# Sample state update in other PSUM banks, a third state buffer, a first chunk without its zero state, and later loads in the last group

## The chip, the cores and the metric

The kernel runs on one core of a Trainium2 chip. The metric is the device time of one execution in microseconds; lower is better. Engines are named as in the profile: PE (matmul) with PEld (its weight loads), DVE (vector), ACT (scalar), POOL (GpSimd) and SP, which only issues DMAs here. ACT issues some DMAs too.

## What is computed

One layer of a hybrid encoder, for a prompt of 2048 frames and for 8 running streams of 16 frames each (the sample). Cut to what matters:

```python
h = rmsnorm(x);  P = h @ w_in                    # q|k|v, z, b, a, B, C, H
# group A, gated delta rule, 4 heads of 128, in chunks; S is the state, zero at the prompt's start
v_new = u - w @ S
o     = (q*exp(g)) @ S + qk @ v_new
S     = S * a_last + k_tail.T @ v_new
o     = rmsnorm(o) * silu(z)
# group B, short convolution
y     = B * causal_dwconv3(C * H)
x     = x + rmsnorm(concat(o, y) @ w_o)
x     = x + rmsnorm((silu(h2 @ w_gate) * (h2 @ w_up)) @ w_down)
```

The sample starts from given states (`state`, 8 streams x 4 heads x 128 x 128) and returns the new ones; the prompt starts from zero.

## The kernel before

The rows are cut into 17 tiles of 128: 0 to 15 are the prompt, 16 is the sample. `GROUPS` puts them into five groups, `[0..3]`, `[4..7]`, `[8..10]`, `[11, 12, 16]`, `[13..15]`. For each group a loop over 28 weight blocks (slots) multiplies the group's rows by one 128-column block of `w_in`, 24 matmul rows per slot (L317: each product is made of three, from a high and a low part), into one of three `dbank`s. A slot has three thirds, and between thirds the loop runs *events*: short pieces of the delta rule, whose times are written in the table `PLAN` (event number = 3 x slot + third). Events past 84 run in the next group. PE's order is what the code says (`manual_schedule`); the other engines, and SP's DMAs, are ordered by a scheduler that simulates the kernel, unless `issue_after` ties an instruction behind another.

The eight PSUM banks of this phase are three `dbank` (blocks), two `tbank` (transposes), two `gbank` and one `obank` (delta rule). Each name is a ring: the next user waits until the last reader of that bank has finished.

- `fetch` / `weights`: SP loads weight block j (1024 KB, from `wsplit`, L287) into a ring of three; a load waits until PE is through with the block three slots back.
- `gate_decay`, `decay_mask`, `decay_scale`: the cumulated decays of a group are turned (L557), written to DRAM by ACT (`grow`, L561), and read back by SP, broadcast over the partitions, into `dt` (L563); DVE adds masks (L569), ACT takes the exponential (L572), DVE scales (L576). `pair_keys` (L592 on PE, L593 on DVE) uses `dt`.
- `chunk`: one prompt tile of the delta rule: products with S (L739, L747), with the solved U (L755), the new S (L761, L764) and the output (L769, L770); `out_norm`, `out_turn` (L720, L722) finish it. The first chunk of the prompt runs the same code on `S_init`, which DVE zeroes at the start.
- `sample_head`: one head of the sample. Its state `st` (512 KB) is loaded by SP (L793), multiplied (L806), solved (L812), used (L816), and updated: four matmuls (L824) into four banks, `pss = [bank(), bank(), obank(), tbank()]`, then eight DVE operations (L826) that read two halves of each bank; ACT stores it (L828).
- `ahead`: in the last group, loads the first quarter of `w_o` and the first output tile's inputs into parts of `U`, `AU`, `dt`, `kt`, `vt`, `sz` that are free (256 KB each, L905 to L909). The event is at 64, but the scheduler may place the issues earlier.

After the five groups come the output projection (L1116), the gated up-projection (L1351) and the down-projection (L1528).

Of the kernel before, what the change touches and what calls it, by code (L numbers as in the profile page):

```python
# [9 lines left out]
F32 = mybir.dt.float32  # L10
# [7 lines left out]
P = 128  # L18
D = 1024
KD = D // P  # L20
H = 4
# [4 lines left out]
NS = 8  # L26
# [6 lines left out]
MAXT = max(len(g) for g in GROUPS)  # L33
# [19 lines left out]
NR, NKV, NACC = 3, 2, 3  # L53
XKB = 6
NHX = 1
NWB = 12
NDA = 6
NDR = 4
# [32 lines left out]
def kernel(  # L91
# [66 lines left out]
    with ExitStack() as ph:  # L158
# [6 lines left out]
        def obank():  # L165
            return pso.tile([P, 512], F32, tag="o", name="obank")

        def tbank():
            return pst.tile([P, 512], F32, tag="t", name="tbank")

        def bank():
            return psg.tile([P, 512], F32, tag="g", name="gbank")

        S_init = gp.tile([P, H, P], F32, tag="S", name="S_init", bufs=2)
        V.memset(S_init, 0.0)
        now = {"S": S_init}
        junko = gp.tile([P, P], BF16, name="junko")
        masks = gp.tile([P, 648], F32, name="masks")
        tri_p, tri_s, blk_s, smask, neg_p, neg_s = (masks[:, a - 256:b - 256] for a, b in list(CONSTS.values())[2:])
# [207 lines left out]
        def finish_block(j, ps, g):  # L387
            tiles, n, rb = g["tiles"], g["n"], g["rb"]
            c = n * P
            pc = g["npr"] * P  # L390
            kind, h = BLOCKS[j]
            if kind == "k":
                o = gp.tile([P, W1], F32, tag="kT", name="kT", bufs=H)
                conv_qkv(tiles, 4 + h, ps, o, rb)
                g["kT"].append(o)

                def later():
                    tb, t3 = turned(o, n)
                    sumsq(tb, n, g["ssk"], h)
                    A.copy(g["kt"][:, h, :n], t3)  # L400
                return later
            if kind == "q":
                o = gp.tile([P, W1], F32, tag="qT", name="qT", bufs=H)
                conv_qkv(tiles, h, ps, o, rb)
                g["qT"].append(o)

                def later():
                    tb, _ = turned(o, n)
                    sumsq(tb, n, g["ssq"], h)
                return later  # L410
            if kind == "v":
                raw = cp.tile([P, W1], F32, tag="vraw", name="vraw", bufs=NKV)
                conv_qkv(tiles, 8 + h, ps, raw, rb)

                def later():
                    _, t3 = turned(raw, n)
                    for i in range(n):
                        A.activation(g["vt"][:, h, i], t3[:, i], AF.Copy, scale=g["rt"][:, 4 * i + h:4 * i + h + 1])
                return later
            if kind == "z":  # L420
                src = ps[:, :c]
                if rb is not None:
                    src = g["sz"][:, h, :c]
                    V.tensor_mul(src, ps[:, :c], rb[:, :c])
                mark["A"] = A.activation(g["sz"][:, h, :c], src, AF.Silu)
                flush(mark["A"])
            w = scw[:, h, :]
            v = lambda a: sl(a[:, pc:c])
            if kind == "C":
                g["cs"] = cs = cp.tile([P, W1], F32, tag="cs", name="cs")  # L430
                if rb is None:
                    flush(A.copy(cs[:, :c], ps[:, :c]))
                else:
                    V.tensor_mul(cs[:, :c], ps[:, :c], g["rb2"][:, :c])
            if kind == "H":
                cs = g["cs"]
                g["acc"] = acc = cp.tile([P, WF], F32, tag="acc", name="acc", bufs=NACC)
                u = cp.tile([P, 3 + WF], F32, tag="R", name="u", bufs=NR)
                f = pc
                G.tensor_copy(u[:, 0:2], shist[:, h, :])  # L440
                V.tensor_mul(u[:, 2:2 + pc], cs[:, :pc], ps[:, :pc])
                G.tensor_copy(shist[:, h, :], u[:, pc:pc + 2])
                if pc < c:
                    f = pc + NS * (2 + LS)
                    us = segments(u, pc, 2, 2 + LS)
                    V.tensor_copy(us[:, :, 0:2], sch[:, h])
                    V.tensor_mul(us[:, :, 2:], v(cs), v(ps))
                    V.tensor_copy(sch[:, h], us[:, :, LS:LS + 2])
                mark["A"] = A.activation(acc[:, :f], u[:, 2:2 + f], AF.Copy, scale=w[:, 2:3])
                mark["V"] = taps(acc[:, :f], lambda d: u[:, d:d + f], w, 3)  # L450
            if kind == "B":
                acc = g["acc"]
                last = h == 3 and g["gi"] + 1 == len(GROUPS)
                yo = wk.tile([P, W1], F32, tag="ye", name="yo") if last else cp.tile([P, W1], F32, tag="cs", name="yo")
                V.tensor_mul(yo[:, :pc], acc[:, :pc], ps[:, :pc])
                if pc < c:
                    V.tensor_mul(v(yo), segments(acc, pc, 0, 2 + LS)[:, :, 2:], v(ps))
                if rb is not None:
                    V.tensor_mul(yo[:, :c], yo[:, :c], rb[:, :c])
                if last:  # L460
                    last_stores.append((mixs[g["gi"]][:, h, :], yo[:, :c]))
                else:
                    nc.scalar.dma_start(out=mixs[g["gi"]][:, h, :], in_=yo[:, :c])
# [89 lines left out]
        def gate_decay(g):  # L553
            n, nG = g["n"], g["nG"]
            m = 4 * n
            ps = bank()
            T.transpose(ps[:m, :P], nG[:, :m], ident)  # L557
            rw = small.tile([4 * MAXT, P], F32, tag="rw", name="rw", bufs=1)
            V.tensor_scalar_mul(rw[:m], ps[:m, :P], -1.0)
            grow = dram.tile([4 * MAXT, P], F32, name=f"grow{g['gi']}")  # L560
            nc.scalar.dma_start(out=grow[:m], in_=rw[:m])  # L561
            g["dt"] = dt = gp.tile([P, MAXT, H, P], F32, tag="dt", name="dt")
            nc.sync.dma_start(out=dt[:, :n].rearrange("p t h c -> p (t h) c"), in_=grow[:m].partition_broadcast(P))  # L563

        def decay_mask(g, i):
            dt, nG, t = g["dt"], g["nG"], g["tiles"][i]
# [161 lines left out]
        def tail_keys(g, i):  # L728
# [2 lines left out]
                A.activation(kl[:, h], g["kt"][:, h, i], AF.Copy, scale=g["tl"][:, 4 * i + h:4 * i + h + 1])  # L731
            return kl

        def chunk(g, i):
            c = slice(i * P, (i + 1) * P)
            S = now["S"]
# [52 lines left out]

        def sample_head(g, i, h):  # L790
            c = slice(i * P, (i + 1) * P)
            st = wk.tile([P, NS, P], F32, tag="st", name="st", bufs=2)
            tc.keep_in_program_order(nc.sync.dma_start(out=st, in_=state[:, h].rearrange("s k v -> k s v")))  # L793
            yield
            kz, qz, kl, r, yt, o = (smp[nm] for nm in ("kz", "qz", "kl", "r", "yt", "o"))
# [22 lines left out]
            ye = smp["ye"]  # L818
            V.tensor_mul(ye, yt[h].unsqueeze(1).broadcast_to([P, 2, P]), smp["pair"].unsqueeze(2).broadcast_to([P, 2, P]))
            yield  # L820
            pss = [bank(), bank(), obank(), tbank()]
            for j, ps in enumerate(pss):
                r_ = slice(32 * j, 32 * j + 32)
                T.matmul(ps[:, :2 * P], kl[r_, h, :], ye[r_].rearrange("p s v -> p (s v)"), start=True, stop=True)  # L824
# [15 lines left out]
        def plan(g, nx, events):  # L840
# [33 lines left out]
                at(u + 10, lambda: out_norm(g, npr, smp["o"]))  # L874
                at(u + 17, lambda: out_turn(g, npr, smp["o"]))
            for i in range(npr):
                thread((t, t + 2, t + 4, t + 10), chunk(g, i))
                t += 6
            if nx is not None:
                tiles = GROUPS[gi + 1]  # L880
                m = len(tiles)
                for i in range(m):
                    at(43 + 4 * i, x_rows_load, tiles, i, nx)
                    at(46 + 4 * i, x_rows, i, nx)
                b = 47 + 4 * m + (0 if gi else 3)
                at(b - 3, x_factors, tiles, nx)
                at(b, x_spread, tiles, nx)
                ts = [62, 65, 68, 69, 70, 71, 72, 73]
                for k in range(KD):
                    at(ts[k], x_load, tiles, k, nx)  # L890
                    if k < NHX:
                        at(max(ts[k], b) + 5, x_norm, tiles, k, nx)
                        at(max(ts[k], b) + 6, x_split, tiles, k, nx)
                    else:
                        at(max(ts[k], b) + 6, x_norm, tiles, k, nx)

            else:
                at(64, ahead, g)

        def ahead(g):  # L900
            kt, vt, sz = (g[nm][:, :, MAXT - 1] if nm != "sz" else g[nm][:, :, W1 - P:] for nm in ("kt", "vt", "sz"))
            early_w[:] = [(U[:, MAXT - 1], AU[:, MAXT - 1]), (g["dt"][:, MAXT - 1], kt)]
            for k, halves in enumerate(early_w):
                for q, v in enumerate(halves):
                    nc.sync.dma_start(out=v, in_=w_o[k, :, 512 * q:512 * q + 512].rearrange("p (h c) -> p h c", h=H))  # L905
            early_m[:] = [vt, sz]
            nc.sync.dma_start(out=vt, in_=mixo[0])
            gi, i = PLACE[0]
            nc.sync.dma_start(out=sz, in_=mixs[gi][:, :, i * P:(i + 1) * P])  # L909

        def next_rows(gi, nx):
            tiles = GROUPS[gi]
# [77 lines left out]
        matmuls(firsts[2], pending[2][1:], hi, lo, c, range(6))  # L990
        rb = spread(rg, n)
        matmuls(firsts[2], pending[2][1:], hi, lo, c, range(6, KD))
        rb2 = wk.tile([P, NS, P], F32, tag="st", name="rb2", bufs=2).rearrange("p s v -> p (s v)")[:, :W1]
        G.memset(U, 0.0)

        def constants():
# [727 lines left out]
```

## Time and profile before

| | us |
|---|---|
| median of 3 runs | 2456.97 (2456.92 to 2458.26) |
| span of the profiled execution, first to last instruction | 2457.2 |
| PE busy | 2428.1 |
| DVE busy | 1619.9 |
| ACT busy | 1045.7 |
| POOL busy | 578.6 |

No time of the profiled execution other than its span is listed; the span lies 0.2 us above the median. PE is the engine that sets the time: what it does not do is 29 us. Groups 0 to 4 run to about 860 us (chunk 0 at 173 us, the sample from about 650 to 742 us), the output projection and gated up-projection to about 1980 us, the down-projection to the end. The mean granted clock of PE is 0.998.

### The profile page before, as it was taken

Reading aid. Unit: us, or ns where it says so; the run is one execution under the profiler, and the core shown is the slowest. Engines: PE = TensorE matmul, PEld = TensorE weight load, DVE = VectorE, ACT = ScalarE, POOL = GpSimd, SP = SyncE. Lnnn points to the kernel's source line nnn. Section 1 sums busy time; section 2 is a strip of 40 time slices with the busy share of each in tenths; the row PEclk is TensorE's granted clock in tenths of the full one; section 3 lists DMA queues with packets and bytes.
Section 4 is the critical chain, followed back from the end, with each engine's and each line's share of the span. In section 5 each row is a group of like instructions: output and inputs, shape, how many; then the busy total and the mean of one; then the engine's idle time right before and its main releaser. Section 6 shows DMA issues by size and latency. Waiting matters only on the chain.

```text
span 2457.2 us, 39354 instructions
## 1 busy us (share of the span) xinstructions
PE 2428.1 (99%) x14376; PEld 2222.2 (90%) x14376; DVE 1619.9 (66%) x3079; ACT 1045.7 (43%) x2338; POOL 578.6 (24%) x664
## 2 busy tenths in 40 slices
PE   9999999999999999999999999999999999999997
PEld 7888889999989978899999999999999988887886
DVE  7875755746667366788888644556555565677698
ACT  6545546546444343444444422324333345333343
POOL 1101001001110000156655200000000046455563
PEclk9999999999999999999999999999999999999999
DMA  7774655666776466598877788778898743333465
GB/s 272 262 246 163 220 194 203 244 222 232 273 261 234 162 222 225 195 336 301 289 268 259 266 261 266 252 246 273 307 298 283 249 144 118 116 111 122 132 224 191
DMA packets 263465, 561.38 MB, mean 228 GB/s; under 512 B 25188, under 2 KB 144680, under 8 KB 245992
## 3 DMA queue, kind: packets, MB, share of 16 engines
q1 hardware_dynamic: 146864, 486.98, 57.3%
q10 hardware_dynamic: 116184, 70.85, 9.5%
q8 instruction: 113, 1.85, 0.3%
q0 software_dynamic: 224, 1.05, 0.1%
q14 instruction: 80, 0.66, 0.1%
HBM read 400.09 MB, written 158.70 MB: 227 GB/s over the span
## 4 chain that ended last, share of the span: by engine, by line
PE 87%; DVE 6%; DMA 2%; issue 2%; POOL 2%; ACT 1%; SPq 0%; DVEq 0%; ACTq 0%; POOLq 0%
PE fbank L1351 36%; PE dbank L317 26%; PE fbank L1528 11%; PE dbank L1116 4%; PE tbank L1116 4%; POOL dw L1201 1%; DVE xr L1551 1%; PE tbank L375 1%; DVE acc L1488 1%; PE gbank L592 1%; PE gbank L599 1%; PE obank L769 1%; POOL as L1511 1%; PE obank L747 1%; PE gbank L739 1%
## 5 line engine op out<-in xcount | busy, mean ns | idle before, releaser
L1351 PE MATMUL fbank<-xh,fw 128*128 128x384 f32 (+1 forms) x3696 | 898.1, 326 | 2.7 <-ACT m L1385 2.5
L317 PE MATMUL dbank<-hi,w 128*128 128x384 f32 (+1 forms) x2240 | 655.6, 363 | 2.2 <-DMA w<-wsplit 1.4
L1351 PEld LDWEIGHTS fbank<-xh,fw 128*128 128x128 f32 x3696 | 651.6, 188 | 3.4 <-ACT m L1385 2.8
L1351 PE MATMUL fbank<-xl,fw 128*128 128x384 f32 (+1 forms) x1848 | 602.4, 326 | 0.0
L317 PEld LDWEIGHTS dbank<-hi,w 128*128 128x128 f32 x2240 | 412.6, 188 | 43.9 <-issue 4.0
L1528 PE MATMUL fbank<-dw,as 128*128 128x512 f32 x1782 | 420.2, 392 | 3.4 <-DVE as L1511 1.2
L1528 PEld LDWEIGHTS fbank<-dw,as 128*128 128x128 f32 x1782 | 332.9, 188 | 82.1 <-POOL as L1511 3.5
L317 PE MATMUL dbank<-lo,w 128*128 128x384 f32 (+1 forms) x1120 | 399.6, 357 | 0.3 <-DVE lo L232 0.3
L1351 PEld LDWEIGHTS fbank<-xl,fw 128*128 128x128 f32 x1848 | 347.3, 188 | 0.0
L317 PEld LDWEIGHTS dbank<-lo,w 128*128 128x128 f32 x1120 | 210.7, 188 | 16.6 <-DVE lo L232 0.6
L1511 POOL TENSOR_TENSOR as<-ar,as 128x256 fp32r<-128x256 f32 (+1 forms) x202 | 184.2, 924 | 171.1 <-ACT as L1508 168.7
L1488 DVE TENSOR_TENSOR acc<-acc,fbank 128x512 f32<-128x512 f32 x248 | 164.9, 681 | 90.2 <-PE fbank L1528 77.1
L1201 POOL TENSOR_TENSOR dw<-dr,dw 128x512 fp32r<-128x512 f32 x48 | 70.3, 1477 | 497.5 <-ACT dw L1199 497.3
L1508 ACT CAST as<-ar 128x256 fp32r<-128x256 f32 (+1 forms) x287 | 116.4, 427 | 166.8 <-PE fbank L1528 124.3
L1326 ACT CAST fw<-rg 128x512 fp32r<-128x512 f32 x124 | 77.2, 622 | 228.6 <-PE fbank L1351 138.3
L321 DVE SCALAR_TENSOR_TENSOR acc<-R,vec,acc 128x512 f32<-128x512 f32 (+2 forms) x180 | 120.9, 672 | 27.0 <-ACT acc L358 20.8
L1399 DVE TENSOR_TENSOR c<-u,fbank 128x384 f32<-128x384 f32 (+1 forms) x66 | 34.8, 528 | 95.5 <-PE fbank L1351 95.5
L1395 DVE TENSOR_TENSOR m<-m,m 128x384 f32<-128x384 f32 (+1 forms) x44 | 23.1, 525 | 82.8 <-ACT m L1385 82.8
L1327 POOL TENSOR_TENSOR fw<-rg,fw 128x512 fp32r<-128x512 f32 x44 | 65.3, 1485 | 45.9 <-ACT fw L1326 41.9
L1397 ACT ACTIVATE m<-fbank 128x384 f32<-128x384 f32 (+1 forms) x66 | 31.2, 473 | 96.4 <-PE fbank L1351 79.0
L350 POOL COPY hist<-R 128x3 f32<-128x3 f32 x60 | 20.1, 335 | 220.6 <-ACT R L326 171.5
L1402 ACT ACTIVATE c<-c 128x384 f32<-128x384 f32 (+1 forms) x66 | 33.4, 507 | 83.4 <-DVE c L1401 83.4
(395 smaller groups left out, 3575.6 us busy)
## 6 DMA issues: line engine op xcount, KB each, us to landing
w<-wsplit SPq DMA_DIRECT2D x105, 1024.0 KB, 4.9
fw<-fsplit SPq DMA_DIRECT2D x188, 512.0 KB, 4.8
fsplit<-fw SPq DMA_DIRECT2D x94, 512.0 KB, 3.6
partd<-pt ACTq DMA_DIRECT2D x86, 384.0 KB, 6.1
rg<-in_w_gu SPq DMA_DIRECT2D x62, 512.0 KB, 4.0
wsplit<-w SPq DMA_DIRECT2D x28, 1024.0 KB, 4.9
wr<-in_w_in SPq DMA_DIRECT2D x34, 512.0 KB, 5.8
ar<-partd SPq DMA_DIRECT2D x43, 384.0 KB, 3.1
```

The costliest lines, as they stand in the source:

```text
L317: T.matmul(ps[:, :c], l[:, k, :], r[k][:, :c], start=(k == 0 and r is hi and l is wh), stop=(k == KD - 1 and l is wl))
L321: r = V.scalar_tensor_tensor(acc, raw(d), w[:, d:d + 1], acc, op0=ALU.mult, op1=ALU.add)
L1116: T.matmul(pss[n], m_[:, j, :], w_[k][:, n * 512:(n + 1) * 512], start=(k == 0 and ci == 0), stop=(k == KD - 1 and ci == 2))
L1201: e.tensor_tensor(out=w[1], in0=v, in1=w[0].bitcast(F32), op=ALU.subtract)
L1326: A.copy(w[:, 0], v)
L1327: e.tensor_tensor(out=w[:, 1], in0=v, in1=w[:, 0].bitcast(F32), op=ALU.subtract)
L1351: T.matmul(ps, w_[:, c], b_[k][:, :hw], start=(first and k == 0 and ci == 0), stop=(k == KH - 1 and ci == 2), skip_group_check=not first)
L1399: V.tensor_add(c21, u2, b3)
L1488: return eng.tensor_tensor(out=dst, in0=dst, in1=ps, op=ALU.add)
L1508: ins = A.copy(a[:, 0, :n], v)
L1511: e.tensor_tensor(out=a[:, 1, :n], in0=v, in1=a[:, 0, :n].bitcast(F32), op=ALU.subtract)
L1528: T.matmul(ps, a[:, x_, q * P:(q + 1) * P], w[y_], start=(start and q == 0 and ci == 0), stop=(q == c - 1 and ci == 2), skip_group_check=True)
```

## The change

Five edits:

1. The sample's update uses one `gbank`, both `tbank`s and one `dbank` instead of two `gbank`s, the `obank` and one `tbank`. The first chunk of the sample's group turns its output two events later.
2. The state ring `st` has three buffers instead of two; the last output block `yo` uses that ring too.
3. The first chunk has a function of its own, `first_chunk`, without the two products with S and with copies where the zero state was scaled and added. `S_init` goes.
4. In the last group the decay broadcast is issued by an event of its own, `decay_load`, three events after `gate_decay` and tied behind the newest weight load.
5. `ahead` runs as six events (40, 44, ... 60), one load each, tied behind the newest weight load.

```diff
+NST = 3
...
-        S_init = gp.tile([P, H, P], F32, tag="S", name="S_init", bufs=2)
-        V.memset(S_init, 0.0)
-        now = {"S": S_init}
+        now = {"S": None}
...
-                yo = wk.tile([P, W1], F32, tag="ye", name="yo") if last else cp.tile([P, W1], F32, tag="cs", name="yo")
+                yo = wk.tile([P, NS * P], F32, tag="st", name="yo", bufs=NST)[:, :W1] if last else cp.tile([P, W1], F32, tag="cs", name="yo")
...
-            nc.sync.dma_start(out=dt[:, :n].rearrange("p t h c -> p (t h) c"), in_=grow[:m].partition_broadcast(P))
+            if g["gi"] + 1 < len(GROUPS):
+                decay_load(g)
+
+        def decay_load(g):
+            n = g["n"]
+            with tc.issue_after(wloads[-1].ins) if g["gi"] + 1 == len(GROUPS) else ExitStack():
+                nc.sync.dma_start(out=g["dt"][:, :n].rearrange("p t h c -> p (t h) c"), in_=g["grow"][:4 * n].partition_broadcast(P))
...
+        def first_chunk(g):
+            o = wk.tile([P, H, P], F32, tag="o", name="o", bufs=2)
+            kl = tail_keys(g, 0)
+            yield
+            ps = bank()
+            for h in range(H):
+                T.matmul(ps[:, h * P:(h + 1) * P], U[:, 0, h, :], g["vt"][:, h, 0], start=True, stop=True)
+            yt = wk.tile([P, H, P], F32, tag="yt", name="yt")
+            A.copy(yt, h4(ps))
+            yield
+            ps = bank()
+            for h in range(H):
+                T.matmul(ps[:, h * P:(h + 1) * P], kl[:, h, :], yt[:, h, :], start=True, stop=True)
+            now["S"] = gp.tile([P, H, P], F32, tag="S", name="S", bufs=2)
+            V.tensor_copy(now["S"], h4(ps))
+            ps = obank()
+            for h in range(H):
+                T.matmul(ps[:, h * P:(h + 1) * P], g["dt"][:, 0, h, :], yt[:, h, :], start=True, stop=True)
+            A.copy(o, h4(ps))
+            out_norm(g, 0, o)
+            yield
+            out_turn(g, 0, o)
+            yield
...
-            st = wk.tile([P, NS, P], F32, tag="st", name="st", bufs=2)
+            st = wk.tile([P, NS, P], F32, tag="st", name="st", bufs=NST)
...
-            pss = [bank(), bank(), obank(), tbank()]
+            pss = [bank(), tbank(), tbank(), psd.tile([P, 512], F32, tag="d", name="dbank")]
...
-                thread((t, t + 2, t + 4, t + 10), chunk(g, i))
+                thread((t, t + 2, t + 4, t + (12 if npr < n and not i else 10)), chunk(g, i) if gi or i else first_chunk(g))
...
-                at(64, ahead, g)
+                at(decay + 3, decay_load, g)
+                for q in range(6):
+                    at(40 + 4 * q, ahead, g, q)
```

How this stands in the queues. First PE, where the first head of the sample is updated while the chunk before it is still running (about 682 us), before:

```order
L317 MATMUL dbank<-hi,w_7152 128x384
L824 MATMUL gbank<-dt,AU 128x256 x2
L824 MATMUL obank<-dt,AU 128x256
L824 MATMUL tbank<-dt,AU 128x256
L720 MATMUL tbank<-cst,o 128x128 x4
L761 MATMUL gbank<-yt,kl 128x128 x4
L769 MATMUL obank<-yt,dt 128x128 x4
L317 MATMUL dbank<-hi,w_7195 128x384
```

The same place now (L853 is the update, L790 and L798 are the chunk's last two products, L316 the blocks; the chunk's turn, L720 above, comes after the next head's first products):

```order
L316 MATMUL dbank<-hi,w_7128 128x384
L853 MATMUL gbank<-dt,AU 128x256
L853 MATMUL tbank<-dt,AU 128x256 x2
L853 MATMUL dbank<-dt,AU 128x256
L790 MATMUL gbank<-yt,kl 128x128 x4
L798 MATMUL obank<-yt,dt 128x128 x4
L316 MATMUL dbank<-hi,w_7171 128x384
```

The turn moved back, and the update left the `obank` and one `gbank` to the chunk. Then SP in the last group, from the weight block of slot 4 on (names: `wsplit` is a weight block, `in_w_o`, `mixo` and `mixs` are the early loads, `grow` the decays), before:

```order
L287 DMA w2_7765<-wsplit8_90 128x2048
L907 DMA vt_7660<-mixo0_60 128x4x128
L287 DMA w2_7825<-wsplit9_91 128x2048
L287 DMA w2_7893<-wsplit10_92 128x2048
L905 DMA AU_200<-in_w_o 128x512
L905 DMA dt_8058<-in_w_o 128x512
L287 DMA w2_7964<-wsplit11_93 128x2048
L287 DMA w2_8034<-wsplit12_94 128x2048
L563 DMA dt_8058<-grow4_8056 128x1536
L909 DMA sz_7661<-mixs0_77 128x4x128
L287 DMA w2_8111<-wsplit13_95 128x2048
L287 DMA w2_8153<-wsplit14_96 128x2048
```

The same stretch now:

```order
L286 DMA w2_7741<-wsplit8_90 128x2048
L286 DMA w2_7801<-wsplit9_91 128x2048
L286 DMA w2_7869<-wsplit10_92 128x2048
L286 DMA w2_7940<-wsplit11_93 128x2048
L286 DMA w2_8010<-wsplit12_94 128x2048
L286 DMA w2_8086<-wsplit13_95 128x2048
L568 DMA dt_8034<-grow4_8032 128x1536
L286 DMA w2_8129<-wsplit14_96 128x2048
```

The early loads left this stretch, and the broadcast moved behind `wsplit13`. The early loads (L939, L941) now stand here, some ten slots later on SP:

```order
L286 DMA w2_8413<-wsplit7_89 128x2048
L939 DMA U_197<-in_w_o 128x512
L286 DMA w2_8476<-wsplit16_98 128x2048
L286 DMA w2_8535<-wsplit17_99 128x2048
L939 DMA AU_198<-in_w_o 128x512
L286 DMA w2_8588<-wsplit18_100 128x2048
L939 DMA dt_8034<-in_w_o 128x512
L286 DMA w2_8622<-wsplit19_101 128x2048
L939 DMA kt_7635<-in_w_o 128x4x128
```

They are six loads spread between weight blocks; the last two (vt, sz) follow in the same manner.

More of the change, by code (lines that the diff above doesn't have):

```diff
@@ L561, in gate_decay @@
             nc.scalar.dma_start(out=grow[:m], in_=rw[:m])
-            g["dt"] = dt = gp.tile([P, MAXT, H, P], F32, tag="dt", name="dt")
-            nc.sync.dma_start(out=dt[:, :n].rearrange("p t h c -> p (t h) c"), in_=grow[:m].partition_broadcast(P))
+            g["dt"], g["grow"] = gp.tile([P, MAXT, H, P], F32, tag="dt", name="dt"), grow
+            if g["gi"] + 1 < len(GROUPS):
[4 more added lines that the diff above has]
+                nc.sync.dma_start(out=g["dt"][:, :n].rearrange("p t h c -> p (t h) c"), in_=g["grow"][:4 * n].partition_broadcast(P))
         def decay_mask(g, i):
@@ L897, in plan, with ahead @@
             else:
-                at(64, ahead, g)
-        def ahead(g):
+                at(decay + 3, decay_load, g)
+                for q in range(6):
+                    at(40 + 4 * q, ahead, g, q)
+        def ahead(g, q):
             kt, vt, sz = (g[nm][:, :, MAXT - 1] if nm != "sz" else g[nm][:, :, W1 - P:] for nm in ("kt", "vt", "sz"))
             early_w[:] = [(U[:, MAXT - 1], AU[:, MAXT - 1]), (g["dt"][:, MAXT - 1], kt)]
-            for k, halves in enumerate(early_w):
-                for q, v in enumerate(halves):
-                    nc.sync.dma_start(out=v, in_=w_o[k, :, 512 * q:512 * q + 512].rearrange("p (h c) -> p h c", h=H))
             early_m[:] = [vt, sz]
-            nc.sync.dma_start(out=vt, in_=mixo[0])
             gi, i = PLACE[0]
-            nc.sync.dma_start(out=sz, in_=mixs[gi][:, :, i * P:(i + 1) * P])
+            with tc.issue_after(wloads[-1].ins):
+                if q < 4:
+                    c = slice(512 * (q % 2), 512 * (q % 2) + 512)
+                    nc.sync.dma_start(out=early_w[q // 2][q % 2], in_=w_o[q // 2, :, c].rearrange("p (h c) -> p h c", h=H))
+                else:
+                    nc.sync.dma_start(out=early_m[q - 4], in_=mixs[gi][:, :, i * P:(i + 1) * P] if q > 4 else mixo[0])
         def next_rows(gi, nx):
@@ L992 @@
         matmuls(firsts[2], pending[2][1:], hi, lo, c, range(6, KD))
-        rb2 = wk.tile([P, NS, P], F32, tag="st", name="rb2", bufs=2).rearrange("p s v -> p (s v)")[:, :W1]
+        rb2 = wk.tile([P, NS, P], F32, tag="st", name="rb2", bufs=NST).rearrange("p s v -> p (s v)")[:, :W1]
         G.memset(U, 0.0)
```

## The prediction

> **What bounds the kernel now.** I read four views in this order: the page, the waits of TensorE (PE), the stretches of 50 us, and the order of time around each wait that the change touches. The page first: the engines' busy time.
> ```profile
> PE 2428.1 (99%) x14376; PEld 2222.2 (90%) x14376; DVE 1619.9 (66%) x3079; ACT 1045.7 (43%) x2338; POOL 578.6 (24%) x664
> ```
> PE is busy for 2428.1 of 2457.2 us, so a change can only pay by issuing fewer matmuls or by closing some of the 29 us in which PE stands. The waits of PE say what it stands for; columns are total us, times, longest.
> ```profile
> PE dbank L317 <- DMA w<-wsplit: 1.4, 1, 1.4
> PE gbank L806 <- DVE st L826: 1.2, 1, 1.2
> PE gbank L761 <- DVE st L826: 1.1, 1, 1.1
> PE gbank L806 <- DMA st<-in_state: 0.6, 1, 0.6
> PE obank L769 <- DVE st L826: 0.4, 1, 0.4
> PE fbank L1528 <- DVE as L1511: 0.9, 1, 0.9
> PE fbank L1528 <- DVE acc L1488: 0.8, 1, 0.8
> ```
> The first five lie in the groups with the sample and after it, 1.4 + 1.2 + 1.1 + 0.6 + 0.4 = 4.7 us, and each names a thing that the diff edits. The last two are in the first down-projection chunk (1980 to 2060 us), which the diff does not edit. The stretches agree (first column after the comma: PE busy out of 50).
> ```profile
> 650.00:700.00 50.00, 48.52 (x384) 45.93 (x383) 24.78 (x73) 17.83 (x57) 6.49 (x19) 1.00 0.74 247
> 700.00:750.00 50.00, 48.22 (x358) 44.29 (x357) 33.42 (x94) 26.42 (x58) 7.73 (x22) 1.00 0.82 275
> 750.00:800.00 50.00, 48.53 (x347) 47.85 (x346) 36.81 (x106) 23.01 (x48) 2.09 (x10) 1.00 0.60 218
> 800.00:850.00 50.00, 50.00 (x446) 48.72 (x445) 17.67 (x45) 18.23 (x57) 2.75 (x6) 1.00 0.53 186
> ```
> Holes are 1.48, 1.78 and 1.47 us, then none. After 850 us the same PE-bound work follows, so what PE wins here should stay won.
>
> **First chunk without its zero state.** Eight of PE's calls go, recorded as 16 matmuls (each fp32 one twice).
> ```profile
> 173.31 1.06 PE L739 MATMUL gbank<-S_init,kT 128*128 128x128 f32 x8
> 174.20 1.06 PE L747 MATMUL obank<-S_init,qT 128*128 128x128 f32 x8
> 175.01 0.48 PE L317 MATMUL dbank<-hi,w 128*128 128x512 f32 x1
> 178.50 1.05 PE L755 MATMUL gbank<-r,U 128*128 128x128 f32 x8
> 173.76 0.68 DVE L704 TENSOR_SCALAR U<-gbank 64x512 f32<-64x512 f32 x1
> ```
> From start to start they hold PE from 173.31 to 175.01: 1.7 us, on the path since nothing waits there, so -1.7. What was behind them moves up: the product with U starts at 178.50 - 1.7 = 176.8, and its last input is written by DVE at 173.76 + 0.68 = 174.4, 2.4 us earlier. The DVE and ACT work that goes with the zero state (r, four scalings of o, four updates of S, for one copy each of S and o) and the memset lie beside PE: nothing. Were that cover gone, the 1.7 would shrink by what U came late.
>
> **Sample update in other banks.** Before, one head's update took both g banks, the single o bank and one t bank; now one g, both t and one d bank.
> ```profile
> 682.26 0.48 PE L824 MATMUL gbank<-dt,AU 32*128 32x256 f32 x2
> ...
> 682.91 0.66 PE L720 MATMUL tbank<-cst,o 128*128 128x128 f32 x4
> 684.68 1.13 PE L761 MATMUL gbank<-yt,kl 128*128 128x128 f32 x8 [1.11 <-DVE st L826]
> 686.18 1.13 PE L769 MATMUL obank<-yt,dt 128*128 128x128 f32 x8 [0.37 <-DVE st L826]
> ...
> 702.75 0.65 PE L806 MATMUL gbank<-st,kz 128*32 128x128 f32 x16 [1.22 <-DVE st L826]
> ```
> At these places the next products need a g or o bank that DVE has not read out, because its queue is full there. In the new order the chunk's products find the other g bank and the o bank untouched, and the next head's L806 finds a g bank last read by L817. So -1.11 - 0.37 - 1.22 = -2.7. What is late next? A t bank: the chunk's turn L720 needs one, but is moved two events behind, and DVE had the whole update done by 686.6:
> ```profile
> 685.95 0.60 DVE L826 SCALAR_TENSOR_TENSOR st<-st,eLs,tbank 128x128 f32<-128x128 f32 x2
> 682.93 0.41 DVE L455 TENSOR_TENSOR yo<-acc,dbank 128x256 f32<-128x256 f32 x1
> 758.55 4.18 PE dbank L317 x24
> ```
> And the d banks: of three, one is lent to the sample, so a block's bank must be read out within one block of 24 rows (4.18 us) instead of two. The block that ends just before 682.26 is read by DVE from 682.93, under 2 us after its end. Price: nothing up to 1.2 (the longest wait on L826 seen); I take nothing, nearest that row of 2 us against 4.18.
>
> **Third state buffer.** The load of the fourth head's state waited for a store.
> ```profile
> SPq L793 <- DMA out_state_s<-st: 7.3, 1, 7.3
> 716.93 0.64 PE L806 MATMUL gbank<-st,kz 128*32 128x128 f32 x16 [0.56 <-DMA st<-in_state]
> ```
> With three buffers it takes the first head's, stored a head earlier, so SP need not stand 7.3 us: the state can be asked for as much earlier than it was, lands before PE wants it at 716.93 - 0.56, and -0.56 follows. The weight loads behind it on SP also go out earlier. The buffer for the last output row block moves into the same ring and is free by then: nothing.
>
> **Decay broadcast and early loads.** On SP, in the last group, w13 is the weight block from wsplit13. The chain of waits reads:
> ```profile
> 742.51 0.32 SPq L563 DMA_DIRECT2D dt<-grow  x1
> 743.57 0.55 SPq L909 DMA_DIRECT2D sz<-mixs  x1
> 744.22 8.40 DMA w<-wsplit
> 752.75 0.41 PE L317 MATMUL dbank<-hi,w 128*128 128x384 f32 x1 [1.40 <-DMA w<-wsplit]
> ```
> w13 stood behind the broadcast and behind the early load of sz, and then took 8.40 us, sharing the queues with both. Now it goes ahead of the broadcast, and sz comes some twelve weight blocks later. PE wanted w13 at 752.75 - 1.40 = 751.35, and its buffer is free two blocks of 4.18 earlier, at 743.0 (an estimate); the weight loads of this stretch land after 6.4 us (next fence), so at 749.4, and even 8.40 would be in time. So -1.40. What is late next is dt, which now queues behind 1024 KB:
> ```profile
> DMA packets 8170, 18.22 MB, mean 260 GB/s; under 512 B 557, under 2 KB 5821, under 8 KB 6543
> ...
> w<-wsplit SPq DMA_DIRECT2D x12, 1024.0 KB, 6.4
> 747.38 1.14 DVE L569 SCALAR_TENSOR_TENSOR dt<-dt,nG,masks 128x128 f32<-128x128 f32 x4 [0.41 <-DMA dt<-grow]
> 750.27 2.18 DVE L569 SCALAR_TENSOR_TENSOR dt<-dt,nG,masks 128x128 f32<-128x128 f32 x8
> 757.99 1.29 DVE L593 TENSOR_TENSOR AU<-gbank,dt 128x512 f32<-128x512 f32 x2
> 763.23 1.06 PE L592 MATMUL gbank<-kT 128*128 128x128 f32 x8
> ```
> 1024 + 768 KB at the 260 GB/s of that stretch are 7.1 us: from 743.0 to 750.1 instead of 747.3. The masks (1.14 + 2.18) then end at 753.4 instead of 752.4, and L593, whose first product freed its g bank at about 758.7, does so at 759.7. PE asks for that bank at 763.23 - 1.40 = 761.8: 2.1 us to spare, so nothing. At the worst, with w13's 8.40 and then dt's own 4.9 (742.51 to 747.38) one after the other, dt lands at 756.3, the masks end 7.2 later than before, and PE waits 758.7 + 7.2 - 761.8 = 4.1 us. The six early loads (256 KB each, 1.0 us at 260 GB/s, and about 0.5 us of SP to issue, as sz's 0.55) move between the weight loads of 785 to 845 us, where DMA runs at 186 GB/s and PE has no hole: nothing, with a bound of six times 1.0.
>
> The Trainium skill (DMA: Bandwidth & Descriptors, Queues, rings and completion order) says that each DMA engine consumes descriptors in ring order; by that rule dt's bytes follow w13's, which is the 750.1 above and never w13 and dt sharing the rate from the start. The trace agrees so far as w13 behind dt took 8.40. Taken strictly it speaks against this part: what w13 wins, dt loses, which is the first rival below.
>
> **The sum**: -1.7 - 2.7 - 0.6 - 1.4 = -6.4. After a wait the first matmul also takes longer to start up (1.4 us from the last transposes' pace to L761 where 1.11 is booked), some 0.3 at one or two places, so -6.5. The order of the first down-projection chunk changes a little too (ACT and DVE casts swap; an input load passes a weight load), around the two waits of 0.9 and 0.8: between -1.7 and, if both double, +1.7; I take nothing. The profiled span 2457.2 is 0.2 above the median 2456.97, so I take the sum from 2457.0: **2450.5 us**.
>
> **Rivals.** *The late dt takes over* (rival 1): PE waits at the third pair-keys product, 0 to 4.1 us; taken at 2.5, 2453.0. For it: dt is now behind w13. Against: the 2.1 us of cover, and that the AU and dt loads of w_o no longer run just ahead. *Banks* (rival 2): the d or t bank becomes the wait, each of the four heads losing up to the 1.2 seen, so half the 2.7 or all of it comes back: 2453.2 at most 2454. Against: the 4.18 us of a block. *Early loads starve the weights* (rival 3, slower): seven weight loads stand next to an early load between 785 and 845 us; if each landed like w13 and PE waited 1.4 for each, 9.8 us are lost, 2457.0 - 6.5 + 9.8 = 2460.3. It decides when a weight lands later than two blocks after its issue, 2 x 4.18 = 8.4 us; w13 with 1024 KB ahead of it took exactly that, and these have 256 KB ahead, so I give it little. *Absorbed* (rival 4): the first down-projection chunk's new order gives back its 1.7 or more: 2452.2.
>
> **How the numbers follow.** Forecast 0.62, rival 1 0.12, rival 2 0.08, rival 4 0.14, rival 3 0.04. The forecast's own range is 2448.6 (all startup gaps and the 1.7 of the chunk won) to 2452.2; eight in ten are held by 2447.8 to 2453.6. A measurement of this kernel can tell about 0.2%, 4.9 us, from no change. Faster by more than that means below 2452.1: the forecast nearly whole, and half of rivals 1 and 4, 0.72; within it 0.25; slower 0.03.
>
> **What would show it.** Right: no L739 or L747 on a zero state near 173 us; no wait of PE on L826; none on the state's load; L317 near 750 us without a wait on wsplit; holes of 650 to 800 us below 1 us together. Wrong: a new wait of PE on a d or t bank, on DVE's AU (L593), or on wsplit between 785 and 845 us, or more than 1.7 us of PE waits between 1980 and 2060 us.

## The result and the profile after

Over 22 runs of each kernel on the same chips the median went from 2457.49 us (2454.35 to 2467.16) to 2456.51 us (2450.38 to 2460.86). The ratio is 0.9984, with a 95% interval of 0.9976 to 0.9991: 3.9 us faster, between 2.2 and 5.9. The two medians are only 1.0 us apart, the means of the same runs 3.6 (2458.6 and 2455.0), because the changed kernel's times fall into two groups and its median lies in the upper one; the ratio is near the means. It is a gain, but a smaller one than the 0.2% that the prediction drew as its line. The profiled execution took 2450.9 us (span 2449.1).

The page's line of busy times and the waits of PE in the changed kernel follow. Its line numbers differ: L855 was L826, L845 was L816, L835 was L806, L727 was L722, L477 was L478, L1560 was L1528, L1383 was L1351.

```profile
PE 2425.0 (99%) x14360; PEld 2220.6 (91%) x14360; DVE 1616.3 (66%) x3070; ACT 1047.5 (43%) x2335; POOL 579.5 (24%) x664
```
```profile
PE fbank L1560 <- DVE acc L1520: 3.5, 3, 1.7
...
PE gbank L477 <- DVE st L855: 0.8, 1, 0.8
PE gbank L845 <- ACT qT L842: 0.6, 1, 0.6
```

The 16 matmul records of the zero state are gone. None of the five waits that the change aimed at is left: no wait on `wsplit`, none on the state's load, none of the chunk's two products or of the next head's on the update. But two new ones stand among the sample's heads, 0.8 + 0.6 us: the next group's gate products (L477) wait for the update, and the sample's output product (L845) waits for `yt`, the answer that ACT copies at L842 (the profile gives that row the name of another tile, qT). In the stretches the holes fell from 1.48, 1.78 and 1.47 us to 0.62, 0.81 and 0.07:

```profile
650.00:700.00 50.00, 49.38 (x416) 46.14 (x414) 25.23 (x74) 17.22 (x56) 6.47 (x19) 1.00 0.76 257
700.00:750.00 50.00, 49.19 (x337) 45.96 (x332) 34.80 (x100) 27.82 (x60) 8.07 (x23) 1.00 0.80 263
750.00:800.00 50.00, 49.93 (x446) 49.25 (x445) 37.63 (x105) 22.44 (x48) 2.27 (x11) 1.00 0.67 235
```

To compare kernels I split each span by the starts of PE's rows. *Groups* is from the first to the last block product (L317/L316), *gate-up* from the last output-projection product to the last gate-up product, *down* from there to the last row (a row can hold several products). *Sample* is the part of the groups from the first head's products with its state to the last head's update. The time is the median of the runs, or the one run, and a ratio is to runs of the kernel before on the same chip. Every kernel of the table is described below.

| | groups | sample | gate-up | down | time | ratio, 95% interval |
|---|---|---|---|---|---|---|
| before | 853.7 | 59.5 | 918.7 | 460.0 | 2457.49 | |
| e12_before | 855.2 | 59.4 | 914.5 | 460.0 | 2455.76 | |
| after | 848.6 | 57.6 | 914.5 | 461.1 | 2456.51 | 0.9984, 0.9976 to 0.9991 |
| e11_after | 848.3 | 57.5 | 921.4 | 459.7 | 2456.29 | |
| e1_first | 852.7 | 60.6 | 921.8 | 460.1 | 2457.41 | 1.0003, 0.9994 to 1.0012 |
| e2_banks | 851.1 | 56.9 | 915.2 | 460.2 | 2455.18 | 0.9998, 0.9985 to 1.0010 |
| e3_ring | 853.2 | 58.8 | 916.2 | 459.3 | 2457.52 | 1.0002, 0.9991 to 1.0014 |
| e4_loads | 851.8 | 59.4 | 915.7 | 460.2 | 2454.70 | 0.9994, 0.9983 to 1.0004 |
| e5_two | 849.1 | 57.4 | 915.2 | 460.9 | 2451.63 | |
| e6_free | 849.0 | 58.0 | 915.2 | 460.6 | 2453.45 | 0.9984, 0.9974 to 0.9993 |
| e7_decay | 851.6 | 59.1 | 916.3 | 460.7 | 2455.22 | |
| e8_early | 853.2 | 59.5 | 915.2 | 460.7 | 2455.84 | |
| e9_turn | 848.2 | 56.5 | 915.1 | 461.3 | 2451.43 | 0.9985, 0.9976 to 0.9994 |
| e10_both | 846.6 | 55.7 | 921.4 | 459.9 | 2454.46 | 0.9985, 0.9974 to 0.9995 |

The groups, which the change edits, are 5.1 to 6.9 us shorter, depending on which of the two profiles of before is set against which of after. The gate-up stretch, which no kernel here edits, takes anything from 914.5 to 921.8 us, and hides that in the totals.

### The profile page after: what moved, and what is told of

It reads as the page before. It is cut to its first block, busy times and chain, and to the rows that moved or that the text cites. A ratio compares the mean times of both kernels' runs of the same rounds, so it can differ in the third digit from the quotient of the medians.

```text
span 2449.1 us, 39308 instructions
## 1 busy us (share of the span) xinstructions
PE 2425.0 (99%) x14360; PEld 2220.6 (91%) x14360; DVE 1616.3 (66%) x3070; ACT 1047.5 (43%) x2335; POOL 579.5 (24%) x664
## 4 chain that ended last, share of the span: by engine, by line
PE 88%; DVE 5%; DMA 2%; issue 2%; POOL 2%; ACT 1%; DVEq 0%; ACTq 0%; SPq 0%; POOLq 0%
PE fbank L1383 36%; PE dbank L316 26%; PE fbank L1560 11%; PE dbank L1148 4%; PE tbank L1148 4%; DVE xr L1583 1%; DVE acc L1520 1%; PE tbank L374 1%; POOL dw L1233 1%; PE gbank L597 1%; PE gbank L604 1%; DMA dr<-in_w_dn 1%; PE ftbank L1177 1%; PE obank L776 1%; PE gbank L768 1%
## 5 line engine op out<-in xcount | busy, mean ns | idle before, releaser
L1383 PE MATMUL fbank<-xh,fw 128*128 128x384 f32 (+1 forms) x3696 | 897.2, 326 | 0.2 <-ACT m L1416 0.2
L316 PE MATMUL dbank<-hi,w 128*128 128x384 f32 (+1 forms) x2240 | 655.3, 363 | 1.1 <-DVE w L296 0.5
L1383 PEld LDWEIGHTS fbank<-xh,fw 128*128 128x128 f32 x3696 | 651.1, 188 | 0.6 <-ACT m L1416 0.5
L1383 PE MATMUL fbank<-xl,fw 128*128 128x384 f32 (+1 forms) x1848 | 601.8, 326 | 0.0
L316 PEld LDWEIGHTS dbank<-hi,w 128*128 128x128 f32 x2240 | 412.6, 188 | 42.2 <-issue 3.6
L1560 PE MATMUL fbank<-dw,as 128*128 128x512 f32 x1782 | 419.9, 392 | 4.4 <-DVE acc L1520 2.4
L1560 PEld LDWEIGHTS fbank<-dw,as 128*128 128x128 f32 x1782 | 332.9, 188 | 83.0 <-ACT as L1540 4.7
L316 PE MATMUL dbank<-lo,w 128*128 128x384 f32 (+1 forms) x1120 | 399.6, 357 | 0.5 <-DVE lo L231 0.5
L1383 PEld LDWEIGHTS fbank<-xl,fw 128*128 128x128 f32 x1848 | 346.9, 188 | 0.0
L316 PEld LDWEIGHTS dbank<-lo,w 128*128 128x128 f32 x1120 | 210.7, 188 | 16.8 <-DVE lo L231 0.8
L1417 ACT COPY m<-fbank 128x384 f32<-128x384 f32 (+1 forms) x66 | 30.7, 464 | 75.8 <-PE fbank L1383 73.7
```

Source lines behind the costliest of these rows:

```text
L316: T.matmul(ps[:, :c], l[:, k, :], r[k][:, :c], start=(k == 0 and r is hi and l is wh), stop=(k == KD - 1 and l is wl))
L1383: T.matmul(ps, w_[:, c], b_[k][:, :hw], start=(first and k == 0 and ci == 0), stop=(k == KH - 1 and ci == 2), skip_group_check=not first)
L1560: T.matmul(ps, a[:, x_, q * P:(q + 1) * P], w[y_], start=(start and q == 0 and ci == 0), stop=(q == c - 1 and ci == 2), skip_group_check=True)
```

## The experiments

Theory A is the prediction's own: each part pays its term and nothing is given back. Theory B is read from the trace after: the banks' part gives back 1.4 us in two new waits.

**The parts alone (e1 to e4).** Each is the kernel before with one piece of the diff.

```diff
# e1_first: first_chunk alone
-        now = {"S": S_init}
+        now = {"S": None}
...
# e2_banks: the sample's banks and the later turn
-            pss = [bank(), bank(), obank(), tbank()]
+            pss = [bank(), tbank(), tbank(), psd.tile([P, 512], F32, tag="d", name="dbank")]
...
# e3_ring
+NST = 3
...
# e4_loads: decay_load and the six events of ahead
-                at(64, ahead, g)
+                at(decay + 3, decay_load, g)
+                for q in range(6):
+                    at(40 + 4 * q, ahead, g, q)
...
```

> The kernel before with the first chunk's own function alone. Theory A (each part pays its own term, and nothing is given back elsewhere): the stretch of the five groups, 853.7 us in the kernel before from the first to the last product with the weight blocks, is 1.7 us shorter (852.0), the rest unchanged; 2455.8 against 2457.5. Rival (cover gone): the product of the first chunk with U then waits for ACT or DVE, and the stretch is less than 0.8 us shorter.

> The kernel before with the sample's update in one g, two t and one d bank, and the first chunk's turn two events later, alone. Theory A: the three waits on the update (1.11, 0.37, 1.22 us) go, and the groups take 2.7 us less, 851.0. Theory B (the trace of the changed kernel: two new waits stand there, 0.61 on the answer copied by ACT and 0.81 on the update's g bank): the part pays 2.7 - 1.4 = 1.3, so the groups take 852.4, and both new waits are seen with this part alone.

> The kernel before with the third state buffer alone; the order of every engine's instructions stays as it was. Theory A: the wait of 0.56 us on the fourth head's state goes, groups 853.1. Rival: the wait is not on the state but falls with the bank waits before it, so that with only this part the gap at the fourth head stays at 0.5 or more, groups 853.7.

> The kernel before with the decay broadcast and the six early loads issued later, alone. Theory A: the wait of 1.40 us on wsplit13 near 751 us goes and nothing takes its place, groups 852.3. Rival: the broadcast now behind wsplit13 is late, and PE waits 0.3 to 4.1 us at the third pair-keys product near 763 us, or for a weight block between 785 and 845 us; groups 853.4 to 857.8.

*e1_first* won its 1.7 us at its own place and lost 1.3 of it later. The next group's gate products (L478 before), a mark between the first chunk and the sample, start at 194.89 us before and at 193.42 here; over all kernels the median of that mark is 194.89 without the part and 193.24 with it, 1.65 us. But the wait of the chunk's state product on the update more than doubled (here L783), while SP's weight block 13 was waited for 0.7 instead of 1.4:

```profile
684.50 1.13 PE L783 MATMUL gbank<-yt,kl 128*128 128x128 f32 x8 [2.41 <-DVE st L848]
```

PE was early, but DVE was not: ahead of the update it scales rows that a load brings. Before, then here:

```profile
682.46 0.56 DVE L274 TENSOR_TENSOR xk<-xk,rb 128x384 f32<-128x384 f32 x1 [0.80 <-DMA xk<-in_xT]
```
```profile
682.29 0.56 DVE L272 TENSOR_TENSOR xk<-xk,rb 128x384 f32<-128x384 f32 x1 [2.10 <-DMA xk<-in_xT]
```

DVE goes on at 682.3 to 682.5 in both, so the rows do not come earlier. So neither theory as written holds: PE did win its 1.7, no wait for U's product took it back, and 1.3 of it became a longer wait of DVE for a load, passed on through the g bank 500 us later.

*e2_banks* took away all three bank waits, the 0.56 on the state too, and brought a new one of 0.93 us on the remaining g bank. Its groups are 2.6 us shorter, near theory A's 2.7 and above theory B's 1.3; the wait on `yt` that theory B named does not stand here, so it isn't this part's alone.

```profile
703.05 1.16 PE L478 MATMUL gbank<-xk,wbag 128*32 128x384 f32 x10 [0.93 <-DVE st L826]
```

*e3_ring* won 0.5 us, as expected, and *e4_loads* 1.9 where 1.4 was expected; neither put a wait in place of the one removed. Two profiles of the kernel before differ by 1.5 us in this stretch (e12 below), so these differences in the groups are shown less well than the waits that went. No one of the four could be told from no change by its time.

**Two parts together (e5).** The kernel before with the pieces of e1 and e2.

> The kernel before with the first chunk's function and the sample's other banks together, nothing else. Theory A: the 1.3 us that the wait of the chunk's state product on the sample's update (L783 there) took back from the first chunk's part alone cannot be taken back once the banks are apart: groups 853.7 - 1.7 - 2.6 = 849.4, against 850.1 if the two parts alone (-1.05 and -2.61) simply add. Down-projection: these two together are the least set of the five edits that issues the first down-projection chunk's loads and casts in the new order; if that order costs the 1.0 us, that stage takes 461.1 from the last gate-up product as in the changed kernel, else 460.1 as in the parts alone.

The groups came to 849.1: together the two win 4.6 us, 0.9 more than both alone (1.0 + 2.6). That is nearer theory A's 849.4 than the 850.1 of plain addition, but both are within what two profiles of one kernel differ by. The sample tells more, since it repeats within 0.1 us: 57.4 us here, where the first part alone had made it 60.6. Both new waits stand here with 0.60 each. The one on the g bank comes with the banks alone (e2), the one on `yt` only when PE is early by the first chunk's part too. Down took 460.9 with the new order of the first down-projection chunk; e7 and e8, with the old order, took 460.7, and the changed kernel's second profile 459.7. The profiles do not tell the two orders apart.

**What made weight block 13 late (e7, e8).** Each is the kernel before with half of e4: only the decay broadcast moved, or only the early loads.

> The kernel before with the decay broadcast alone put behind wsplit13; the early loads stay, sz (256 KB) ahead of wsplit13. Queue theory (wsplit13 was late by what stood ahead of it, three quarters of it the broadcast's 768 KB): the wait of 1.40 us near 751 goes whole, groups 852.3. Rival (sz was what made it late): a wait of 0.5 or more on wsplit13 stays.

> The kernel before with the six early loads alone issued later; the decay broadcast stays ahead of wsplit13, sz does not. Queue theory: wsplit13 lands 0.5 us earlier (a quarter of the 2 us by which it was late), a wait of 0.9 us stays near 751, groups 853.2 or, with what the other early loads cost elsewhere, 852.8. Rival (sz was what made it late): no wait, groups 852.3.

With the broadcast behind the block the wait is gone, as in every kernel here that has this edit. With only the early loads moved it is 0.9:

```profile
PE dbank L317 <- DMA w<-wsplit: 0.9, 1, 0.9
```

The 0.9 is what the share of bytes gave, but it proves little: the kernels that leave all these loads in place waited 0.7 (e1, e5), 1.3 (e2, e3), 1.4 (before) and 2.0 us (e12). It does speak against sz as the only cause. The broadcast ahead of the block is thus shown as the cause, the share of sz is not.

The Trainium skill (DMA: Bandwidth & Descriptors, Queues, rings and completion order) says that each DMA engine consumes descriptors in ring order; e7, where the block goes first and is in time, agrees with it.

**Taking the new waits away (e6).** The changed kernel, with two edits.

```diff
         def gate_parts(nx, n):
             c = n * P
-            ps = bank()
+            ps = obank()
...
-            A.copy(yt[h], ps[:, :P])
+            V.tensor_copy(yt[h], ps[:, :P])
```

> The changed kernel with its two new waits taken away: the next group's gate products (L477) take the o bank instead of the g bank that the update holds, and the sample's answer yt is copied by DVE instead of ACT (L842). Theory B (these two are all that the banks' part gave back): the 0.81 and the 0.61 us go, and the groups take 1.4 us less than the changed kernel's, 847.1. Rival: DVE, which is behind with the update and the casts there, is later with the copies than ACT at one of the other heads, or another bank is the next wait; 0.5 us or less is won.

Theory B fell, the rival came: both waits went, and two others of 0.81 and 0.52 us took their place, again on DVE. The groups took 849.0 us against 848.6 and 848.3 of the changed kernel, so nothing was won.

```profile
699.00 0.48 PE L853 MATMUL tbank<-dt,AU 32*128 32x256 f32 x1 [0.81 <-DVE ot L727]
...
705.67 0.49 PE L841 MATMUL gbank<-vt,U 128*128 128x128 f32 x2 [0.52 <-DVE vt L836]
```

This suggests that banks are only where DVE's lateness shows; e9 and e10 below test it. The wait on `yt` too leads back to DVE, by the trace: in the changed kernel ACT, which copies it, stood for DVE's `o`, which is queued behind the first head's update, and then had the squares and scalings of that `o` to do up to 692.7, ahead of the copy at 693.03:

```profile
688.25 0.31 ACT L714 ACTIVATE junko<-o 128x128 bf16<-128x128 f32 x1 [9.34 <-DVE o L799]
...
693.03 0.26 ACT L842 COPY qT<-gbank 128x128 f32<-128x128 f32 x1
```

And DVE is late although it stands. Its rows just before the second head's update, in the changed kernel:

```profile
695.27 0.28 DVE L446 TENSOR_TENSOR u<-cs,dbank 128x128 f32<-128x128 f32 x1
697.48 0.75 DVE L727 SCALAR_TENSOR_TENSOR ot<-tbank,vec,sz 128x512 f32<-128x512 f32 x1 [1.93 <-PE dbank L316]
...
701.43 0.60 DVE L855 SCALAR_TENSOR_TENSOR st<-st,eLs,gbank 128x128 f32<-128x128 f32 x2
```

The row names a block product as the releaser, but L727 reads a t bank that PE had filled by 695.4 (L725, 694.73 + 0.60). What L727 also needs is its output buffer. This is the turn of the group's second chunk; `ot` has one buffer, and ACT issued the store of the first chunk's turn, the one that the edit moved two events back, at 691.55. The time to landing of the two stores of `ot` here is in the second fence; the one issued at 691.55 took the 5.8:

```profile
691.55 0.33 ACTq L729 DMA_DIRECT2D mixo<-ot  x1
```
```profile
DMA to landing us min/median/max: 4.3/5.1/5.8
```

691.55 + 5.8 is 697.4. That gave a third theory. Other traces say the same: in e6 this turn stood 3.48 us, to 698.19, and its store, issued at 690.89, took 7.2 us; so e6's wait on the t bank is the store's too. In e2 the row itself names the store (in e5 also, with 1.74):

```profile
698.36 0.75 DVE L722 SCALAR_TENSOR_TENSOR ot<-tbank,vec,sz 128x512 f32<-128x512 f32 x1 [2.13 <-DMA mixo<-ot]
```

In the kernel before that store was issued at 687.24, and the second turn, at 697.90, did not wait for it.

**The store (e9, e10).** The edit below is e9's, in the changed kernel; e10 adds e6's copy by DVE to it. The output of the sample group's first chunk then takes no `ot`.

```diff
-            ot = wk.tile([P, H, P], F32, tag="ot", name="ot")
+            ot = o if g["npr"] < g["n"] and not i else wk.tile([P, H, P], F32, tag="ot", name="ot")
```

> The changed kernel with one edit: the turned output of the sample group's first chunk is written over o, which is free by then, and not into the single ot buffer. Theory C (in the changed kernel DVE stands 1.9 us before 697.48 for the store of the ot before, issued by ACT at 691.55; this makes the update late, and the bank waits are its consequence): the 1.9 us go, the update of the second head is done that much earlier, and the wait of L477 on it (0.81 us) goes; the wait of 0.61 on yt, which ACT copies, stays: groups 0.8 us shorter than the changed kernel's. Rival: DVE's queue there is full whatever its start, or it stood for something else; L477 still waits 0.5 or more.

> As e9_turn, and the sample's yt is copied by DVE instead of ACT. Theory C: both waits go, 0.81 + 0.61, and unlike in e6_free no other bank takes their place, since DVE is 1.9 us less behind: groups 1.4 us shorter than the changed kernel's, total 2449 to 2455 against 2450 to 2457. Rival: as in e6_free another wait on DVE (t bank on the turn, L841 on r) takes the place; 0.5 or less is won.

Theory C holds. L727 no longer stands in either, with DVE's order there as in the changed kernel apart from e10's copy. The update of the second head begins at 699.87 in e9, 1.6 us earlier than in the changed kernel, and in e10 3.0 us earlier:

```profile
694.40 0.75 DVE L727 SCALAR_TENSOR_TENSOR ot<-tbank,vec,sz 128x512 f32<-128x512 f32 x1
...
698.40 0.60 DVE L855 SCALAR_TENSOR_TENSOR st<-st,eLs,gbank 128x128 f32<-128x128 f32 x2
```

In e9 the wait of L477 is gone, that on `yt` stays at 0.5, and the sample takes 1.1 us less. Its groups are only 0.4 shorter, not the 0.8 expected: the mark of e1 lies at 193.91 there, 0.5 later than in the changed kernel, ahead of anything that e9 edits. In e10 both are gone, the sample takes 1.9 us less and the groups 846.6, the shortest of all, and PE stands 0.07 us between 650 and 800:

```profile
650.00:700.00 50.00, 50.00 (x421) 46.94 (x419) 28.71 (x84) 18.12 (x56) 8.10 (x24) 1.00 0.75 257
700.00:750.00 50.00, 50.00 (x343) 47.01 (x342) 32.95 (x96) 27.60 (x57) 6.19 (x18) 1.00 0.82 279
750.00:800.00 50.00, 49.93 (x448) 49.03 (x447) 38.14 (x103) 20.66 (x46) 2.26 (x11) 1.00 0.63 222
```

By their times neither can be told from the changed kernel (0.9985 against 0.9984, with intervals 0.0015 to 0.0021 wide): the two microseconds are shown in the stage's profile, not in the total. The lowest times are 2448.72 and 2447.93 against 2450.38, but e6, which won nothing in the stage, has 2448.05.

**Both kernels again (e11, e12).**

> The changed kernel once more, for how far one profile can be trusted. If the stretches are the kernel's own: groups 848.6, output projection 202.9, gate-up 914.5, down 461.1, each within 0.5. Rival: the gate-up stretch differs by 1 to 7 us from profile to profile (914.5 to 921.8 in the kernels so far, none of which edits it), and the groups by 0.5 at their start.

> The kernel before once more. If its gate-up stretch of 918.7 is its own, it is 918.7 again and the change gained there; if it is the run's, it is nearer 915.5. The groups 853.7 and down 460.0 each within 0.5.

The rivals hold. The same changed kernel took 921.4 in the gate-up stretch instead of 914.5, and the kernel before 914.5 instead of 918.7. So the wait of 2.5 us on ACT (L1351) that the first profile of before shows is the run's, not the kernel's. The groups of before repeated within 1.5 us only: 0.9 of it lies ahead of the mark after the first chunk, and the wait on weight block 13 was 2.0 instead of 1.4.

## Why the prediction was right and wrong

- *First chunk, -1.7*: right, 1.65 by the mark. Alone, 1.3 of it was lost at the sample's banks (e1); that an earlier PE meets a load that isn't earlier was not in the working.
- *Banks, -2.7, and state, -0.6*: the mechanism was right, the size was not. All four waits went, but the sample is 1.9 us shorter, not 3.3. "What is late next" was answered with t and d banks, and rival 2 named the same two. In the changed kernel neither became a wait (in e6 a t bank did). It was the one g bank that is left and the copy of `yt`, and behind both DVE. The step that failed is "nothing up to 1.2 (...); I take nothing": it looked at how fast DVE reads banks that were read on time before, and not at what DVE itself waits for. The edit moved the first chunk's turn two events back. Its store then frees the only `ot` buffer at 697.4, and the second chunk's turn, which stands for that, is ahead of the second head's update in DVE's queue. e10 shows that the missing 1.4 us are there to be had.
- *Decay and early loads, -1.4*: right. The wait on block 13 went, 1.4 to 2.0 us in the two profiles of before. Block 13 was issued at 739.72, near the estimated 743.0 less the 3.4 us by which the work was ahead by then (the last update of the sample starts at 723.93 instead of 727.28). The broadcast behind it was there at 747.35, 7.6 us after the block's issue (7.1 worked out), and PE did not wait for what hangs on it. Rival 1 did not come:

```profile
739.72 0.32 SPq L286 DMA_DIRECT2D w<-wsplit  x1
740.13 0.39 SPq L568 DMA_DIRECT2D dt<-grow  x1
```
```profile
747.35 3.24 DVE L574 SCALAR_TENSOR_TENSOR dt<-dt,nG,masks 128x128 f32<-128x128 f32 x12 [0.42 <-DMA dt<-grow]
```

- *Early loads starve the weights* (rival 3): no wait on a weight block between 785 and 845 us, nor anywhere from 640 to 860. *Absorbed* (rival 4): PE's waits in the first down-projection chunk are 1.7 + 0.9 us, above the 1.7 that the prediction named as a sign of being wrong. But the second profile of before has 1.4 + 0.9 in the old order, and the stage took 461.1 and 459.7 in the two profiles of after, against 460.0 twice. It isn't shown that the new order costs anything.
- *The signs*: three of the five signs of being right came (the products on a zero state, the wait on the state's load and that on `wsplit` are gone). Two did not: L477 waits for the update, and the holes from 650 to 800 us are 0.62 + 0.81 + 0.07 = 1.5 us, not below 1.
- *The sum*: -6.5 predicted. The marks give -1.65 - 1.9 - 1.4 to 2.0 = -5.0 to -5.6; the groups -5.1 to -6.9; the ratio of the runs -3.9, with -5.9 as the far end of its interval.
- *The time*: the profiled run's 2450.9 met the 2450.5, but by luck: of the 8.1 us between the two profiled spans 4.2 lie in the gate-up stretch, which the change does not edit and which went the other way in the second profiles. The median of 2456.5 lies outside the range of 2447.8 to 2453.6. The step that failed is "so I take the sum from 2457.0". As a median it was good (2457.49 over the 22 runs), but one time minus one sum leaves out what the run itself adds. The profiled execution of before held 918.7 us of gate-up where that kernel can do it in 914.5, and the changed kernel has 9 runs of 2450.4 to 2453.3 and 13 of 2455.5 to 2460.9. The range had no term for it. Three times within 1.3 us had looked like a steady kernel.

## What to carry to other kernels

When an edit takes a wait away, ask what the engine named as releaser was itself waiting for; freeing a buffer in front of a late engine moves the wait to the next buffer (e6), freeing the engine ends it (e10). A releaser that had long been done hides another one, here the landing of a store whose only buffer is to be written again; another kernel's trace can name it outright (e2). Where stages that the change leaves alone vary by more than it can win, compare the stage and its marks, take two profiles of the same kernel before trusting one, and give the range a term for the rest.

## What the runs showed of the hardware

One kernel's gate-up stretch comes out either near 915 us or 4 to 7 us longer. In the two profiles of the changed kernel the same copy on ACT (L1415) comes 1.2 us later in the longer one at 1369 us, and 6.7 us later from 1398 us to the end. Between the two, in the longer one, ACT stands 4.67 us for a store by the trace, and PE then for ACT:

```profile
1378.98 0.37 ACTq L1420 DMA_DIRECT2D partd<-a  x1
1379.38 0.51 ACT L1306 CAST xh<-fh 128x384 fp32r<-128x384 f32 x1 [4.67 <-DMA partd<-pt]
...
1396.01 0.48 ACT L1417 COPY m<-fbank 128x384 f32<-128x384 f32 x1 [1.90 <-DVE pt L1446]
```
```profile
PE fbank L1383 <- ACT m L1417: 2.5, 1, 2.5
PE fbank L1383 <- ACT m L1415: 1.5, 2, 0.9
```

The same wait of 2.5 us near 1395 to 1402 us stands in all four profiles with a long gate-up stretch (before, e1_first, e10_both, e11_after) and in none with a short one. At the same place ACT stands 3.5 to 4.7 us for the store in those four, and at most 1.7 in the others. In the longer profile of the changed kernel the stores of `pt` were also issued later, from 1362.44 instead of 1358.56, so a late landing isn't told from a late issue. Why stays open; no kernel here was made to tell.
